# Attention layer with key and value products first and one query split; opening with zero matmuls, row-block products, half weights and stacked gate halves

## The chip, the cores and the metric

The kernel runs on one core of a Trainium2 chip. The metric is the device time of one execution in microseconds (us). TensorE is called PE below (PEld is its loading of weights), VectorE DVE, ScalarE ACT, GpSimd POOL and SyncE SP.

## The reference: a decoder trunk of two layers

x is 512 tokens of 1024 numbers, float32. Layer 1 is a gated linear attention (GLA, 4 heads of 128 keys and 256 values, in chunks of 64 tokens), layer 2 an attention with 16 heads of 64 in 4 groups. Each is followed by a feed-forward of 2 x 2816 with a short convolution. Cut to what the change touches:

```python
hn = rmsnorm(x, norm_mix[0])
q, k, v, r, a_low = split(hn @ gla_w_in)
log_a = log_sigmoid(a_low @ w_alpha_up + b_alpha) / 16   # a_low: 16 wide
b = cumsum(log_a)                                        # inside each chunk
state = state * exp(b_last) + (k * exp(b_last - b)).T @ v
o = (q * exp(b)) @ state + decayed causal attention inside the chunk
x = x + (rmsnorm(o) * silu(r)) @ w_o
x = x + conv_ffn(rmsnorm(x))

kv = (rmsnorm(x, kv_norm) @ w_kv)                 # 6 sets of 4 groups x 64
k_cmp = gelu(blocks(kv[0]) @ wk1) @ wk2           # 31 blocks of 32 tokens
v_cmp = gelu(blocks(kv[1]) @ wv1) @ wv2
k_sel, k_win = rope(kv[2]), rope(kv[4]);  v_sel, v_win = kv[3], kv[5]

hn = rmsnorm(x, norm_mix[1])
q = hn @ w_q;  gates = sigmoid(hn @ w_g)          # 3 gates per head
x = x + (gates[0] * o_cmp + gates[1] * o_sel + gates[2] * o_win) @ w_o
x = x + conv_ffn(rmsnorm(x));  return rmsnorm(x, norm_final)
```

The two norms ahead of the second attention are of the same x and differ only in their gain.

## The kernel before

**Numbers.** x stands transposed in `xall`, as eight tiles of 128 features x 512 tokens. To keep float32 precision, every operand of a product is split into two parts that PE takes in one pass each: a rounded one (`w_h`, `x_h`; made by ACT) and the rest (`w_l`, `x_l`; by DVE). A product of a 128-column weight with x is then 24 matmuls of 128x512: high by high, low by high, high by low, for each of eight tiles (`mm3`, L222; `proj`, L228; `proj_tok`, L236, has tokens on the partitions). `load_w` (L143) fetches and splits a weight. The gain of a norm is put into x when it is split (`split_x`, L161). The factor 1/rms is applied to the product's result (`rb`, a row spread over all partitions), so products start before the norm is known: `squares` (L188) makes and adds the squares, `rms_cols` sums them over partitions with PE (into `pc`), and `rms_behind` (L211) lets one product run while that is under way.

**Opening and GLA** (`gla`, L354). SP issues all loads: first columns of gains, x tile 0, the decay weight `gla_a` (16 columns), x tiles 1 to 4, the key weight of head 0, x tiles 5 to 7, its query weight, constants `kc`. The decay product `pa` (16 columns, 24 matmuls) and the key product `pk` of head 0 run tile by tile as x comes. ACT and POOL share the squares of this first norm (POOL multiplies those of odd tiles); in the later norms POOL makes the adds of the first tiles. `alow` (16 x 512) times `wup` (16 x 512, one 128-column piece per head) gives `pz`, the log of the decay before the sigmoid, as a plain float32 product, which PE takes in two passes (L383). `head_in` (L381) makes the decay `g`, its running sums `cum`, `k` and `q` of a head; `head_att` (L406) the attention in a chunk; `v_head` (L515) the values with `v_h` and `v_l`. L564 to L592 order the heads.

**Second attention** (`nsa_att`, L612). Its schedule is written out by hand (L901 to L945). x is split by the gain of the query norm (`mix1`), two query products run, x is split again by `kv`; then come rope of query pair 0 (`queries`, L659: SP copies halves over, the copies `q_s` are made by four DMAs), the gates, the rotated keys (`keys_in`, L678), the raw keys and values (`raw_in`, L754, which makes the blocks `kb`), the compression of both (`compress`, L704), scores of head 0, and the values by token (`values_in`, L692; `pvt`, `V`). Then x is split by `mix1` a second time for the later queries. `compressed` (L769) is the compressed branch of a group (`pC`, `pcm`, `smc`), `compressed_t` (L791) transposes its weights, `scores` (L799) has maxima `nm` and exponentials `p_t`, `values` (L854) transposes `p_t` and multiplies by V. In the loop over 16 heads, the scores of head h+1 are interleaved with the values of head h.

**Order.** The code is traced in this order; each engine takes its instructions in order, apart from `tc.high_priority` (moves a piece ahead by an offset) and `tc.issue_after` (not before a given instruction of the same engine). Tiles of one tag share a small ring of buffers (`TAGS`, L51), so that a write waits for the readers of the tile before. The core of the hand-written schedule:

```python
query()
xk = [split_x("kv")]
queries(0)
gates()
keys_in(0)
query()
raw_in(0)
keys_in(1)
raw_in(1)
raw_in(2)
raw_in(3)
compress("k")
compress("v")
run(scores(0))
```

## Time and profile before

| | |
|---|---|
| median of 3 runs | 1347.9 us (1347.73 to 1348.26) |
| profiled execution, its own time | 1346.67 us |
| its span | 1344.9 us |
| PE busy | 98%, 6592 instructions |
| DVE, ACT, POOL busy | 68%, 46%, 13% |
| DMA | 119.79 MB, mean 89 GB/s |

The span runs from the first to the last instruction that the profiler saw; the execution's own time is 1.8 us longer. A matmul's recorded duration covers its way through a pipeline, so two in a row overlap: the time that one costs on a full PE is the distance between two starts. A share of busy time is an average over the whole span; which wait ends last in a stage is read from that stage's rows in order of time.

### The profile page before, as it was taken

What the parts mean: (1) busy time and instruction counts of PE and PEld (TensorE: products, weight loads), DVE (VectorE), ACT (ScalarE), POOL (GpSimd) and SP (SyncE); (2) the same over time, 40 slices, a digit from 0 to 9 for tenths busy, and PEclk for the clock granted to TensorE, in tenths of its full rate; (3) what the DMA queues carried; (4) which work ended last, traced back from release to release, by engine and by line L of the source; (5) the groups of instructions that cost most, each with busy time, mean ns of one, the idle gap of its engine ahead of it and who ended that gap; (6) DMA issues with size and microseconds to landing.
All of it is one profiled execution on the core that took longest, in us unless ns stands there. A gap on an engine that the chain in (4) does not pass through costs nothing. (4 is left out here: it accounts for less than half of the span.)

```text
span 1344.9 us, 17502 instructions
## 1 busy us (share of the span) xinstructions
PE 1316.5 (98%) x6592; PEld 1079.7 (80%) x6592; DVE 911.4 (68%) x1414; ACT 620.4 (46%) x1036; POOL 168.6 (13%) x236
## 2 busy tenths in 40 slices
PE   8999999999999999999989999999999999999997
PEld 4988988888888888887779777777788888888886
DVE  6877765477636763765875898998767735773672
ACT  5444543344314431444446687776644413441342
POOL 3000001100000000002413444442200000000000
PEclk9999999999999999999999999999999999999999
DMA  5222213333333333334452211111333333332331
GB/s 185 73 63 64 63 48 94 95 94 94 94 94 94 98 102 95 94 83 150 121 174 72 65 39 36 48 52 32 112 94 100 103 94 94 94 94 95 94 110 63
DMA packets 40261, 119.79 MB, mean 89 GB/s; under 512 B 5344, under 2 KB 6240, under 8 KB 40176
## 3 DMA queue, kind: packets, MB, share of 16 engines
q1 hardware_dynamic: 39600, 117.62, 29.0%
q8 instruction: 52, 0.85, 0.3%
q10 hardware_dynamic: 576, 1.05, 0.2%
q14 instruction: 33, 0.27, 0.1%
HBM read 109.21 MB, written 2.10 MB: 83 GB/s over the span
## 5 line engine op out<-in xcount | busy, mean ns | idle before, releaser
L149 ACT ACTIVATE w_h<-w_raw 128x1024 fp32r<-128x1024 f32 (+3 forms) x198 | 200.1, 1011 | 307.1 <-PE pd L226 129.9
L224 PE MATMUL pu<-x_h,w_h 128*128 128x512 f32 x704 | 274.1, 389 | 0.0
L225 PE MATMUL pu<-x_h,w_l 128*128 128x512 f32 x704 | 274.1, 389 | 0.0
L226 PE MATMUL pu<-x_l,w_h 128*128 128x512 f32 x704 | 273.9, 389 | 0.0
L151 DVE TENSOR_TENSOR w_l<-w_raw,w_h 128x1024 fp32r<-128x1024 f32 (+3 forms) x184 | 220.0, 1196 | 49.9 <-ACT w_h L149 48.0
L224 PEld LDWEIGHTS pu<-x_h,w_h 128*128 128x128 f32 x704 | 132.1, 188 | 27.5
L226 PEld LDWEIGHTS pu<-x_l,w_h 128*128 128x128 f32 x704 | 132.1, 188 | 27.4
L225 PEld LDWEIGHTS pu<-x_h,w_l 128*128 128x128 f32 x704 | 132.1, 188 | 27.4
L224 PE MATMUL pd<-m_h,w_h 128*128 128x512 f32 x304 | 120.2, 395 | 0.0
L226 PE MATMUL pd<-m_l,w_h 128*128 128x512 f32 x304 | 120.1, 395 | 0.0
L225 PE MATMUL pd<-m_h,w_l 128*128 128x512 f32 x304 | 120.0, 395 | 0.0
L273 DVE TENSOR_TENSOR u<-pu,rb 128x512 f32<-128x512 f32 x88 | 60.6, 689 | 81.3 <-PE pu L226 77.4
L251 DVE TENSOR_TENSOR xall<-xall,pd 128x512 f32<-128x512 f32 x40 | 27.5, 688 | 100.8 <-PE pd L226 100.8
L272 POOL MEMSET u<- 128x2 f32 x88 | 8.4, 99 | 602.5 <-DVE cv L278 602.5
L156 ACT ACTIVATE m_h<-cv 128x512 fp32r<-128x512 f32 x44 | 27.8, 632 | 115.2 <-DVE cv L281 115.2
L275 ACT ACTIVATE cv<-u,cols 128x512 f32<-128x512 f32 x88 | 71.1, 808 | 2.7 <-DVE u L273 1.9
L826 ACT ACTIVATE p_t<-sc,nm 128x128 f32<-128x128 f32 (+3 forms) x128 | 66.8, 527 | 11.0 <-DVE nm L819 7.5
L224 PEld LDWEIGHTS pd<-m_h,w_h 128*128 128x128 f32 x304 | 57.1, 188 | 14.0 <-ACT m_h L156 0.4
L226 PEld LDWEIGHTS pd<-m_l,w_h 128*128 128x128 f32 x304 | 57.1, 188 | 13.9 <-DVE m_l L158 0.2
L278 DVE SCALAR_TENSOR_TENSOR cv<-u,cols,cv 128x512 f32<-128x512 f32 x88 | 66.2, 752 | 3.0
L225 PEld LDWEIGHTS pd<-m_h,w_l 128*128 128x128 f32 x304 | 57.1, 188 | 13.7
L277 DVE SCALAR_TENSOR_TENSOR cv<-u,cols,cv 128x512 f32<-128x512 f32 x88 | 65.7, 746 | 3.6 <-ACT cv L275 3.4
(284 smaller groups left out, 2661.5 us busy)
## 6 DMA issues: line engine op xcount, KB each, us to landing
w_raw<-in_ffn_up_dram SPq DMA_DIRECT2D x88, 512.0 KB, 3.6
w_raw<-in_ffn_down_dram SPq DMA_DIRECT2D x32, 512.0 KB, 3.5
w_raw<-in_gla_v_dram SPq DMA_DIRECT2D x8, 512.0 KB, 3.6
w_raw<-in_gla_r_dram SPq DMA_DIRECT2D x8, 512.0 KB, 3.5
w_raw<-in_gla_o_dram SPq DMA_DIRECT2D x8, 512.0 KB, 3.6
w_raw<-in_nsa_q_dram SPq DMA_DIRECT2D x8, 512.0 KB, 3.6
w_raw<-in_kv_f_dram SPq DMA_DIRECT2D x8, 512.0 KB, 3.8
q_s<-q_s SPq DMA_DIRECT2D x32, 128.0 KB, 2.2
```

What stands on the lines that cost most here:

```text
L149: ACT.activation(h, raw, AF.Copy)
L151: (POOL if pool else DVE).tensor_tensor(l, raw, h, OP.subtract)
L156: ACT.activation(h, src, AF.Copy)
L224: MM.append(PE.matmul(ps, wh, xh, start=first, stop=False).ins)
L225: PE.matmul(ps, wl, xh, start=False, stop=False)
L226: PE.matmul(ps, wh, xl, start=False, stop=last)
L251: DVE.tensor_tensor(xT[d], xT[d], ps, OP.add)
L273: DVE.tensor_tensor(u[:, 2:], ps, rb[0], OP.mult)
L275: ACT.activation(c, u[:, 2:2 + S], AF.Identity, scale=col(w, 3 * jj + 2), bias=col(f"conv_b{layer}", jj))
L277: DVE.scalar_tensor_tensor(c, u[:, 1:1 + S], col(w, 3 * jj + 1), c, OP.mult, OP.add)
L278: DVE.scalar_tensor_tensor(c, u[:, 0:S], col(w, 3 * jj), c, OP.mult, OP.add)
L826: ACT.activation(pr[i, b], scv[:, bi], AF.Exp, bias=nm[:, i, b:b + 1], accum_out=su[:, i, b:b + 1])
```

## The change

**Opening.** Three loads go to ACT's own queue ahead of its table load: the gains and the first halves (four row blocks) of the key and query weights of head 0. The rest stays on SP, with the second halves ahead of x tile 4 and the constants last, and four copies of the decay weight `w_alpha` at partitions 0, 32, 64, 96. Fourteen bf16 matmuls of zeros, 128x512, into the tile `pc` come first on PE. The products go by row block: for each x tile, those of the decay, of the key of head 0 and of its query. The decay weight is stacked to 112 columns (three copies of its high part and, at 96, its low part), so that `pa` takes two matmuls for each tile in place of three; `alow` and `wup` are stacked to match, and `pz` is one matmul of one pass over 112 rows. The key product of head 1 follows, and `rb` is spread behind its second block. All squares are made by ACT and all their adds by DVE, in every norm.

On PE, in the opening before the change (`pa` the decay product, `pk` that of the keys of head 0):

```order
L225 MATMUL pa<-x_h,w_l 16x512
L226 MATMUL pa<-x_l,w_h 16x512
L224 MATMUL pk<-x_h,w_h 128x512
L224 MATMUL pa<-x_h,w_h 16x512
L225 MATMUL pa<-x_h,w_l 16x512
L225 MATMUL pk<-x_h,w_l 128x512
L226 MATMUL pk<-x_l,w_h 128x512
```

And now, behind the zero matmuls (`pk_137` and `pq_138` are keys and queries of head 0):

```order
L393 MATMUL pa<-x_h,wa 112x512
L393 MATMUL pa<-x_l,wa 112x512
L230 MATMUL pk_137<-x_l,wk_h 128x512
L228 MATMUL pq_138<-x_h,w_h 128x512
L229 MATMUL pq_138<-x_h,w_l 128x512
L230 MATMUL pq_138<-x_l,w_h 128x512
L393 MATMUL pa<-x_h,wa 112x512
```

The decay product has one matmul fewer per tile, and the query product, which stood behind the norm, is now part of the same sweep over x.

On DVE, where the inputs of heads 0 and 1 are made, before (`alow` the decay's low-rank part, `g` the decay, `cum` its sums; the second `g` is that of head 1):

```order
L375 TENSOR_TENSOR alow<-pa,rb 16x512
L400 TENSOR_TENSOR k<-pk,rb 128x512
L390 TENSOR_SCALAR g<-pz,cols 128x512
L403 SCALAR_TENSOR_TENSOR q<-pq,rb 128x512
L151 TENSOR_TENSOR w_l<-w_raw,w_h 128x1024
L391 TENSOR_TENSOR g<-g,e 128x512
L395 SCALAR_TENSOR_TENSOR cum<-scan_174,g 128x512
L395 SCALAR_TENSOR_TENSOR cum<-scan_177,g 128x512
L395 SCALAR_TENSOR_TENSOR cum<-scan_180,g 128x512
L390 TENSOR_SCALAR g<-pz,cols 128x512
```

And now:

```order
L413 TENSOR_TENSOR alow_f<-pa,rb 112x512
L445 TENSOR_TENSOR k<-pk_137,rb 128x512
L448 SCALAR_TENSOR_TENSOR q<-pq_138,rb 128x512
L420 TENSOR_TENSOR alow<-alow_f,alow 16x512
L445 TENSOR_TENSOR k<-pk,rb 128x512
L155 TENSOR_TENSOR w_l<-w_raw,w_h 128x1024
L435 TENSOR_SCALAR g<-pz,cols 128x512
L436 TENSOR_TENSOR g<-g,e 128x512
L440 SCALAR_TENSOR_TENSOR cum<-scan_319,g 128x512
L440 SCALAR_TENSOR_TENSOR cum<-scan_322,g 128x512
L440 SCALAR_TENSOR_TENSOR cum<-scan_325,g 128x512
```

`q` of head 0, `k` of head 1 and a low part of a weight now stand ahead of the first `g`.

**Second attention.** x is split by the `kv` gain first. All products of keys and values are made from it (raw, compressed keys, rotated keys, values by token), and then x is split once by `mix1`, for gates and queries. The compression of the values, the gates and the second query product stand behind that. `compressed_t(0)` is moved into the first head.

On DVE, around the last split of x, before (`V_5060` one of the two value tiles, `pcm` and `smc` the softmax of the compressed branch, `nm`, `su` and `p_t` that of head 0):

```order
L697 SCALAR_TENSOR_TENSOR V_5061<-pvt,rc,V_5061 128x4x64
L778 TENSOR_TENSOR pcm<-pC,kc 128x512
L781 TENSOR_REDUCE mx<-pcm 128x16
L819 TENSOR_REDUCE nm<-sc 128x2 x2
L168 SCALAR_TENSOR_TENSOR x_l<-xall,cols,x_h 128x512
L819 TENSOR_REDUCE nm<-sc 128x1
L785 TENSOR_REDUCE smc<-pcm 128x16
L168 SCALAR_TENSOR_TENSOR x_l<-xall,cols,x_h 128x512
L786 RECIPROCAL smc<-smc 128x16
```

And now:

```order
L742 SCALAR_TENSOR_TENSOR V_5090<-pvt,rc,V_5090 128x4x64 x3
L172 SCALAR_TENSOR_TENSOR x_l<-xall,cols,x_h 128x512 x3
L155 TENSOR_TENSOR w_l<-w_raw,w_h 128x1024
L172 SCALAR_TENSOR_TENSOR x_l<-xall,cols,x_h 128x512 x4
L742 SCALAR_TENSOR_TENSOR V_5089<-pvt,rc,V_5089 128x4x64
L155 TENSOR_TENSOR w_l<-w_raw,w_h 128x384
L742 SCALAR_TENSOR_TENSOR V_5089<-pvt,rc,V_5089 128x4x64 x2
L172 SCALAR_TENSOR_TENSOR x_l<-xall,cols,x_h 128x512
L699 SCALAR_TENSOR_TENSOR qn<-sc,rb 128x512
```

The parts of x stand between copies of values and parts of weights, and no softmax work is among them.

The diff, cut:

```diff
+WARM = 14
...
     xall = const.tile([128, KT, S], F32, name="xall")
     xT = [xall[:, k] for k in range(KT)]
-    ACT.preload_act_table_set("natural_log_exp_and_others")
     pre = [T([128, 8, n], F32, "w_raw") for n in (16, 128, 128)]
     kc = const.tile([128, 128 + 128 + 128 + 1], F32, name="kc")
+    for dst, src in ((cols[:, 0:NGAIN], a["cols"][:, 0:NGAIN]), (pre[1][:, 0:4], a["gla_k"][0][:, 0:4]),
+                     (pre[2][:, 0:4], a["gla_q"][0][:, 0:4])):
+        nc.scalar.dma_start(dst, src)
+    ACT.preload_act_table_set("natural_log_exp_and_others")
     for dst, src in ((xT[0], a["xT"][0]), (pre[0], a["gla_a"]), (xT[1], a["xT"][1]), (xT[2], a["xT"][2]),
-                     (xT[3], a["xT"][3]), (xT[4], a["xT"][4]), (pre[1], a["gla_k"][0]), (xT[5], a["xT"][5]),
-                     (xT[6], a["xT"][6]), (xT[7], a["xT"][7]), (pre[2], a["gla_q"][0]), (kc, a["kc"]),
+                     (xT[3], a["xT"][3]), (pre[1][:, 4:8], a["gla_k"][0][:, 4:8]),
+                     (pre[2][:, 4:8], a["gla_q"][0][:, 4:8]), (xT[4], a["xT"][4]), (xT[5], a["xT"][5]),
+                     (xT[6], a["xT"][6]), (xT[7], a["xT"][7]), (kc, a["kc"]),
                      (cols[:, NGAIN:], a["cols"][:, NGAIN:])):
         nc.sync.dma_start(dst, src)
...
-    def load_w(src, shape, raw=None, pool=False):
+    def load_w(src, shape, raw=None, pool=False, prio=300):
         if raw is None:
             raw = T(shape, F32, "w_raw")
             nc.sync.dma_start(raw, src)
-        with tc.high_priority(offset=300):
+        with tc.high_priority(offset=prio):
...
-    def squares(first=False):
+    SQ = []
+
+    def squares():
         acc = None
         for k in range(KT):
-            sq = T([128, S], F32, "sq0" if first else "sq")
-            if first and k % 2:
-                POOL.tensor_tensor(sq, xT[k], xT[k], OP.mult)
-            else:
-                ACT.activation(sq, xT[k], AF.Square)
+            sq = T([128, S], F32, "sq")
+            last = [ACT.activation(sq, xT[k], AF.Square).ins]
             if acc is not None:
-                (POOL if k < 6 and not first else DVE).tensor_tensor(sq, sq, acc, OP.add)
+                last.append(DVE.tensor_tensor(sq, sq, acc, OP.add).ins)
             acc = sq
+        SQ[:] = last
         return acc
...
-        wa, wk, wq = (load_w(None, [128, 8, 128 if i else 16], t) for i, t in enumerate(pre))
-        xs = split_x("mix0")
-        acc = squares(first=True)
...
+        with tc.high_priority(offset=300):
+            zero = T([128, S], BF, "zero")
+            DVE.memset(zero, 0.0)
+            idle = P("pc")
+            for _ in range(WARM):
+                PE.matmul(idle, zero[:, 0:128], zero, start=True, stop=True)
+
+        was = [T([128, 4, 112], F32R, "wa") for _ in range(2)]
+        for wa in was:
+            POOL.memset(wa.bitcast(F32), 0.0)
+        wup_f = T([112, S], F32, "wup_f")
+        POOL.memset(wup_f, 0.0)
+        for o in range(0, 112, 32):
+            nc.sync.dma_start(wup_f[o:o + 16], a["w_alpha"])
+        wk, wq = ([T([128, 8, 128], F32R, n + x) for x in "hl"] for n in ("wk_", "w_"))
+        pa, pk0, pq0 = (P(n) for n in ("pa", "pk0", "pq0"))
+        xs = []
+        for k in range(KT):
+            xs += split_x("mix0", (k,))
+            if k % 4 == 0:
+                for raw, (h, l) in zip(pre[1:], (wk, wq)):
+                    ACT.activation(h[:, k:k + 4], raw[:, k:k + 4], AF.Copy)
+                    DVE.tensor_tensor(l[:, k:k + 4], raw[:, k:k + 4], h[:, k:k + 4], OP.subtract)
+                    if k == 0 and raw is pre[1]:
+                        for i, wa in enumerate(was):
+                            w3 = bass.AP(tensor=wa.tensor, offset=wa.offset,
+                                         ap=[list(wa.ap[0]), list(wa.ap[1]), [32, 3], [1, 16]])
+                            half = pre[0][:, 4 * i:4 * i + 4]
+                            ACT.activation(w3, half[:, :, None, :].to_broadcast([128, 4, 3, 16]), AF.Copy)
+                            DVE.tensor_tensor(wa[:, :, 96:112], half, wa[:, :, 0:16], OP.subtract)
+        acc = squares()
+        r4 = rms_cols(acc)
+        for k in range(KT):
+            for x in xs[k]:
+                PE.matmul(pa[0:112], was[k // 4][:, k % 4], x, start=k == 0 and x is xs[0][0], stop=k == KT - 1 and x is xs[k][1])
+            for ps, (wh, wl) in ((pk0, wk), (pq0, wq)):
+                mm3(ps, (wh[:, k], wl[:, k]), xs[k], k == 0, k == KT - 1)
+        first = len(MM)
+        pk1 = proj(None, xs, "pk", w=load_w(a["gla_k"][1], [128, 8, 128], prio=0))
+        with tc.high_priority(offset=100), tc.issue_after(MM[first + 1]):
+            rb = spread(r4, "rb")
...
-        wup = T([16, S], F32, "wup")
-        nc.sync.dma_start(wup, a["w_alpha"])
...
-        pa = proj(None, xs, "pa", w=wa, m=16)
-        rb, r4 = rms(acc)
-        al = T([16, S], F32, "alow")
-        DVE.tensor_tensor(al, pa[0:16], rb[0:16], OP.mult)
+        al_f = T([112, S], F32, "alow_f")
+        DVE.tensor_tensor(al_f, pa[0:112], rb[0:112], OP.mult)
+        wup = T([112, S], F32R, "wup")
+        with tc.issue_after(SQ[0]), tc.issue_after(SQ[1]):
+            ACT.activation(wup, wup_f, AF.Copy)
+            DVE.tensor_tensor(wup[32:48], wup_f[32:48], wup[32:48], OP.subtract)
+        al = T([112, S], F32R, "alow")
+        ACT.activation(al, al_f, AF.Copy)
+        DVE.tensor_tensor(al[64:80], al_f[64:80], al[64:80], OP.subtract)
...
-            pk = proj(a["gla_k"][h], xs, "pk", w=wk if h == 0 else None)
+            pk = proj(a["gla_k"][h], xs, "pk") if h > 1 else (pk0, pk1)[h]
             k = T([128, S], F32, "k")
             DVE.tensor_tensor(k, pk, rb, OP.mult)
-            pq = proj(a["gla_q"][h], xs, "pq", w=wq if h == 0 else None)
+            pq = proj(a["gla_q"][h], xs, "pq") if h else pq0
             q = T([128, S], F32, "q")
             DVE.scalar_tensor_tensor(q, pq, 128 ** -0.5, rb, OP.mult, OP.mult)
...
-        xq = [split_x("mix1")]
+        xk = split_x("kv")
         acc = squares()
-        early = [proj(a["nsa_q"][0], xq[0], "tp")]
-        rb, r4, ps = rms_behind(acc, lambda: proj(a["nsa_q"][1], xq[0], "tp"))
-        early.append(ps)
+        first = [proj(a["kv_f"][0], xk, "sc")]
+        rb, r4, ps = rms_behind(acc, lambda: proj(a["kv_f"][1], xk, "sc"))
+        first.append(ps)
...
-            ps = early[len(Q)] if len(Q) < 2 else proj(a["nsa_q"][len(Q)], xq[0], "pl", pool=True)
+            ps = proj(a["nsa_q"][len(Q)], xq, "pl" if len(Q) > 1 else "sc", pool=len(Q) > 1)
...
-            ps = proj(a["kv_f"][f], xk[0], "sc")
+            ps = proj(a["kv_f"][f], xk, "sc") if f > 1 else first[f]
...
+        for f in range(4):
+            raw_in(f)
+        keys_in(0)
+        compress("k")
+        keys_in(1)
+        values_in(1)
+        values_in(0)
+        xq = split_x("mix1")
         query()
-        xk = [split_x("kv")]
+        compress("v")
+        gates()
+        query()
         queries(0)
-        gates()
-        keys_in(0)
-        query()
-        raw_in(0)
-        keys_in(1)
-        raw_in(1)
-        raw_in(2)
-        raw_in(3)
-        compress("k")
-        compress("v")
         run(scores(0))
         queries(1)
-        values_in(1)
-        values_in(0)
-        xq[0] = split_x("mix1")
         compressed(0)
         query()
-        compressed_t(0)
         for h in range(16):
             gs = scores(h + 1) if h + 1 < 16 else None
             if h % 4 == 2 and h < 14:
                 compressed(h // 4 + 1)
             gv = values(h)
-            for c in INTERLEAVE:
+            for n, c in enumerate(INTERLEAVE):
+                if h == 0 and n == 6:
+                    compressed_t(0)
                 if c == "v":
...
```

## Rows read from the trace of the kernel before

**Rows 1.** The page's first part: busy time, share of the span, instructions.

```profile
PE 1316.5 (98%) x6592; PEld 1079.7 (80%) x6592; DVE 911.4 (68%) x1414; ACT 620.4 (46%) x1036; POOL 168.6 (13%) x236
```

**Rows 2.** Order of time, PE, opening: start, duration (us), line, operation.

```profile
5.08 0.61 PE L224 MATMUL pa<-x_h,w_h 128*16 128x512 f32 x1 [5.08 <-ACT w_h L149]
...
8.49 0.63 PE L225 MATMUL pa<-x_h,w_l 128*16 128x512 f32 x1
8.92 0.63 PE L226 MATMUL pa<-x_l,w_h 128*16 128x512 f32 x1
...
22.16 1.04 PE L204 MATMUL pc<-mean_d,sq 128*128 128x1 f32 x8
...
26.75 1.12 PE L383 MATMUL pz<-alow,wup 16*128 16x512 f32 x2
27.80 0.50 PE L225 MATMUL pq<-x_h,w_l 128*128 128x512 f32 x1
...
40.99 0.39 PE L226 MATMUL pq<-x_l,w_h 128*128 128x512 f32 x1
41.21 0.28 PE L224 MATMUL pv<-w_h,x_h 128*128 128x256 f32 x1
...
53.54 0.61 PE L438 MATMUL plv<-ev 128*128 128x128 f32 x4
...
56.53 0.39 PE L224 MATMUL pv<-w_h,x_h 128*128 128x256 f32 x1
```

**Rows 3.** PE's waits, 600 to 770 us: total, times, longest (us).

```profile
PE sc L815 <- DVE kb L759: 4.2, 1, 4.2
PE pl L224 <- ACT x_h L166: 1.6, 1, 1.6
PE sc L225 <- DVE w_l L151: 0.9, 1, 0.9
...
PE sc L226 <- DVE x_l L168: 0.5, 1, 0.5
```

**Rows 4.** Order of time, PE, attention stage; in brackets the idle time before it.

```profile
694.61 0.47 PE L815 MATMUL sc<-K,q_s 128*128 128x512 f32 x1 [4.23 <-DVE kb L759]
```

**Rows 5.** Windows: PE, PEld, DVE, ACT, POOL busy (instructions), PE clock, DMA share, GB/s.

```profile
28.63:56.44 27.81, 27.25 (x171) 23.93 (x169) 23.21 (x41) 13.60 (x24) 0.00 (x0) 1.00 0.25 76
695.00:700.00 5.00, 5.00 (x31) 4.85 (x30) 3.55 (x10) 1.74 (x3) 0.00 (x0) 0.66 0.77 266
746.70:960.00 213.30, 208.29 (x1195) 158.96 (x1194) 186.72 (x374) 156.33 (x391) 81.50 (x73) 1.00 0.17 44
```

**Rows 6.** SP's issue of the constants, its landing (page's DMA issues), x_l in the opening.

```profile
6.91 0.70 SPq L122 DMA_DIRECT2D kc<-in_kc_dram  x1
...
kc<-in_kc_dram SPq DMA_DIRECT2D x1, 192.5 KB, 7.0
...
L168 DVE SCALAR_TENSOR_TENSOR x_l<-xall,cols,x_h x8: 737/752/1523, 4.9 to 14.9; 128x512 fp32r<-128x512 f32 x8
```

**Rows 7.** Order of time, DVE, opening: the adds of squares and g of head 0.

```profile
19.09 3.01 DVE L197 TENSOR_TENSOR sq<-sq,sq 128x512 f32<-128x512 f32 x4
...
28.63 0.75 DVE L390 TENSOR_SCALAR g<-pz,cols 128x512 f32<-128x512 f32 x1 [1.48 <-ACT e L386]
```

**Rows 8.** The page's costliest groups: total busy, mean ns of one, idle before.

```profile
L151 DVE TENSOR_TENSOR w_l<-w_raw,w_h 128x1024 fp32r<-128x1024 f32 (+3 forms) x184 | 220.0, 1196 | 49.9 <-ACT w_h L149 48.0
```

**Rows 9.** Query 0: DVE's qn, SP's four issues of q_s, their landing (page).

```profile
630.90 0.69 DVE L654 SCALAR_TENSOR_TENSOR qn<-tp,rb 128x512 f32<-128x512 f32 x1 [2.86 <-ACT rb L178]
...
639.48 5.08 SPq L671 DMA_DIRECT2D q_s<-q_s  x4
...
q_s<-q_s SPq DMA_DIRECT2D x32, 128.0 KB, 2.2
```

**Rows 10.** The chain that ended last, 665 to 688 us: a slow rope's first and last piece.

```profile
667.59 0.70 DVE kx L682
...
683.41 0.61 DVE rot L632
```

More of the change, by code (lines that the diff above doesn't have):

```diff
@@ L48 @@
                ("conv_w0", 132), ("conv_w1", 132), ("conv_b0", 44), ("conv_b1", 44)])
-TAGS = {"sq0": "y1", "x_h": "xs", "x_l": "xs", "kx": "pt_h", "gz": "pt_h", "lo": "sq", "o_t": "sq", "w2": "sq", "qn": "qo", "o_h": "qo", "o_l": "qo", "kb": "qo",
+TAGS = {"sq0": "y1", "x_h": "xs", "x_l": "xs", "zero": "rv", "wa": "ev", "wk_h": "ah", "wk_l": "al", "wup_f": "sqo", "alow_f": "sqo", "pk0": "po", "pq0": "po", "kx": "pt_h", "gz": "pt_h", "lo": "sq", "o_t": "sq", "w2": "sq", "qn": "qo", "o_h": "qo", "o_l": "qo", "kb": "qo",
         "pz": "ps", "pvt": "tp", "pqk": "ps", "plv": "ps", "pc": "pn", "pb": "pn", "pgt": "pn", "pC": "pn", "pT": "pn",
@@ L111, in tile_kernel @@
     cols = const.tile([128, NCOLS], F32, name="cols")
-    nc.sync.dma_start(cols[:, 0:NGAIN], a["cols"][:, 0:NGAIN])
     xall = const.tile([128, KT, S], F32, name="xall")
     xT = [xall[:, k] for k in range(KT)]
-    ACT.preload_act_table_set("natural_log_exp_and_others")
     pre = [T([128, 8, n], F32, "w_raw") for n in (16, 128, 128)]
     kc = const.tile([128, 128 + 128 + 128 + 1], F32, name="kc")
+    for dst, src in ((cols[:, 0:NGAIN], a["cols"][:, 0:NGAIN]), (pre[1][:, 0:4], a["gla_k"][0][:, 0:4]),
+                     (pre[2][:, 0:4], a["gla_q"][0][:, 0:4])):
+        nc.scalar.dma_start(dst, src)
+    ACT.preload_act_table_set("natural_log_exp_and_others")
     for dst, src in ((xT[0], a["xT"][0]), (pre[0], a["gla_a"]), (xT[1], a["xT"][1]), (xT[2], a["xT"][2]),
-                     (xT[3], a["xT"][3]), (xT[4], a["xT"][4]), (pre[1], a["gla_k"][0]), (xT[5], a["xT"][5]),
-                     (xT[6], a["xT"][6]), (xT[7], a["xT"][7]), (pre[2], a["gla_q"][0]), (kc, a["kc"]),
+                     (xT[3], a["xT"][3]), (pre[1][:, 4:8], a["gla_k"][0][:, 4:8]),
+                     (pre[2][:, 4:8], a["gla_q"][0][:, 4:8]), (xT[4], a["xT"][4]), (xT[5], a["xT"][5]),
+                     (xT[6], a["xT"][6]), (xT[7], a["xT"][7]), (kc, a["kc"]),
                      (cols[:, NGAIN:], a["cols"][:, NGAIN:])):
@@ L159, in split, with split_x @@
         return h, l
-    def split_x(gain):
+    def split_x(gain, ks=range(KT)):
         xs = []
-        for k in range(KT):
+        for k in ks:
             g = col(gain, k)
@@ L637, in gates @@
         def gates():
-            pg = proj(a["nsa_g"], xq[0], "po", m=48)
+            pg = proj(a["nsa_g"], xq, "po", m=48)
             gz = T([48, S], F32, "gz")
@@ L679, in keys_in @@
             for ft in range(2):
-                ps = proj(a["kv_f"][4 + 2 * br + ft], xk[0], "sc")
+                ps = proj(a["kv_f"][4 + 2 * br + ft], xk, "sc")
                 k = T([128, S], F32, "kx")
@@ L692, in values_in @@
         def values_in(br):
-            pv = proj_tok(a["kv_v"][br], xk[0], "pvt")
+            pv = proj_tok(a["kv_v"][br], xk, "pvt")
             for i in range(4):
```

## The prediction

> **What bounds the kernel now.** I read the page's first part, then the view of waits, then TensorE's rows in order of time, then the windows. The page shows TensorE (PE) busy for 98% of the span [rows 1], so a gain needs PE work removed or a PE pause closed; what other engines do counts where PE waits for it. Three places matter to this change. In the **opening**, PE has its first product at 5.08 us, and products of 512 columns start 0.43 us apart there (8.49, 8.92), against 0.22 to 0.23 later (40.99, 41.21), which is the 2.4 GHz level; the slow step is the 1.2 GHz level, after 5 us with nothing to do [rows 2]. The value products of head 0 start at 41.21. In the **attention stage**, the view of waits names 4.2 us for kb, 1.6 us for x_h, 0.9 for w_l and 0.5 for x_l [rows 3]; the first is one hole of 4.23 us that ends at 694.61 [rows 4]. Behind that hole the granted clock averages 0.66 over 695 to 700 [rows 5]: a share s at half speed gives 1 - s/2 = 0.66, so s = 0.68, or 3.4 us at half speed, which costs 1.7 us more. The feed-forward stages show no PE wait that the change touches.
>
> **The change part by part.**
>
> *Opening, PE.* The fourteen zero products wait for one clear on VectorE alone; I let them start at 1.1 us, a guess that shifts the sum by its own error only. In the old kernel the slow stretch lasted from 5.08 to past 8.92, ten products [rows 2]; ten zeros at 0.43 and four at 0.23 end near 6.3. From there the eight row blocks (two for the decay, three for k, three for q) are 64 products of 0.23, and the mean-square product has its slot after 61 of them: 6.3 + 14.0 = 20.3. Whether PE gets there without holes depends on x. More weights now stand ahead of the last x tile, but the constants behind them all landed by 13.9 in the old kernel (next paragraph but one), with the same bytes ahead, and PE wants the last tile only at 6.3 + 7 x 1.8 = 18.9. If zeros did nothing for the clock, ten real products would pay 0.2 us more each, 2.0 in all.
>
> The Trainium skill, "TensorE: Matmul & The Clock Gate", section "What's actually happening", says that the number of slow products at the start varies from run to run, with 6, 11 and 14 in one kernel. No run here shows such a spread; by that rule the zeros end between 5.5 and 7.1 instead of at 6.3, which would move the opening by under a microsecond either way.
>
> *Opening, VectorE.* This queue is the later one. All seven adds of squares are now on DVE, none of the squares is made on POOL, and the three casts of the constants stand in front of x_l of tile 5. Those constants landed 7.0 us after their issue at 6.91 [rows 6], at 13.9; the bytes ahead of them are the same now, so I keep 13.9 and let the casts end at 14.4. Behind them stand three x_l of 0.75 [rows 6], six adds of 0.75 (four took 3.01 [rows 7]) and one w_l of 1.2 [rows 8]: 14.4 + 2.3 + 4.5 + 1.2 = 22.4. The mean-square product starts there and not at 20.3; the hole is 2.1 us.
>
> From that product (22.16 in the old kernel) to the value products at 41.21 was 19.05 us. The new one has 14 full products fewer in it (51 for 65), 3.2 us, and two decay products in one pass: the old one takes 1.05 us, 26.75 to 27.80 [rows 2], the new one 0.23, so 0.8 less each. That is 19.05 - 3.2 - 1.6 = 14.2, and the values start at 36.6, 4.6 us earlier. k of head 1 now stands ahead of the scans, and with it goes the old pause inside the values: they took 12.33 us, 41.21 to 53.54, for 96 products of 256 columns, 11.5 at half a product each and a little. PE would be 4.6 + 0.8 = 5.4 us earlier at 53.54.
>
> It keeps less than that. At 56.53 PE takes a value product whose buffer comes free with the second v_l [rows 2]. Between g at 28.63 [rows 7] and that v_l's end at 56.44, DVE was busy 23.21 of 27.81 us [rows 5]. Two w_l (2.4) and one k and one q (1.4) are moved ahead of g, which leaves 19.4, with 0.9 of waits for ScalarE's exponentials 20.3. g itself comes 1.9 us behind the first decay product (at 26.75 before; now 24 products and two decay products ahead of the values, 36.6 - 5.5 - 0.5 = 30.6), at 32.5, so the second v_l ends at 52.8 and PE is 3.6 us ahead at that mark. **I take 3.6**; the bounds are 2 (constants or x land 2 us later) and 7 (the constants land early, and DVE is not late).
>
> *Decay products of heads 2 and 3.* 0.8 us each on a full PE: **1.6**. The copies for the stacked halves lie on ScalarE and DVE beside PE work and cost nothing while DVE keeps its slack: 23.21 of 27.81 us.
>
> *Adds of squares in the later norms* (POOL to DVE, five adds at 0.75 in each of three norms): hidden; PE is full of output products while each x tile waits for its sum. Without that cover it would be 3.8 us each.
>
> *Attention stage.* The raw key and value products come first, so each kb has a whole product of 5.5 us (24 x 0.23) before its buffer is wanted again, and the blocks are formed long before the compression reads them. That closes the 4.2 us hole and the 1.7 of slow clock behind it. One of three splits of x is gone, which removes the x_l wait of 0.5. The remaining split follows the last value product, with no softmax work queued between its parts; the query product takes 5.5 us to come to the tile that is split last. That closes the 1.6 for x_h. The 0.9 for w_l came from a DVE queue full of rope and kb work, which is now spread out. Sum 8.9.
>
> New waits: the value products of the second pair want both buffers, freed by four copies that ScalarE and DVE do beside 3 us of compression products: an estimated 0.5. The first scores lost their cover, the value products. Query 0 now ends about 17.5 us of PE work before the scores (gates 5.5, compression 4.4 and its second product 1.7, query 1 5.5, transpositions 0.4). The old chain from qn at 630.90 to the last copy of q_s, issued by 644.56 and landing 2.2 us later, was 15.9 us [rows 9]: it fits by 1.6, and the first head needs only half the copies. Between scores and first transposition stands the third query, 5.0 us, where DVE has maxima, sums and scalings; I put 1.5 on that start. With 0.5 and 1.5 the stage gives **6.9**; the bounds are 1 (the new waits cost 8) and 10.5 (none, and the small pauses of the old start go as well).
>
> **Sum.** 3.6 + 1.6 + 6.9 = 12.1. The profiled execution took 1346.67 (span 1344.9, 1.8 around it): 1334.6. The median of the runs, 1347.9, is 1.2 above that execution, so 1335.8.
>
> **Rivals.**
> - *The opening gives nothing but shorter products.* DVE stays late through all of head 0 (in its favour: it is in order, and I already find it 2 us behind PE twice; against: it has 4.6 us of slack in that window). Opening 0.5 for 3.6: 1338.9.
> - *The attention stage only moves its pauses.* Rope copies, softmax of the first head and the transposition of the compressed weights stop PE for 7 us in place of 2: 1335.8 + 5 = 1340.8. For it: a rope of the old stage took from 667.59 to 683.41 [rows 10], 15.8 us against 7.2 for the first one, when copies stood behind other transfers. Against: SP has fewer large transfers around query 0.
> - *Slower: the first head runs bare.* If query 0's rope is as slow as that one, PE stops 8.6 - 1.6 = 7 us ahead of the scores, pays 1.7 for the clock behind it, and then waits for a whole head of DVE work, 186.72 / 16 = 11.7 us [rows 5], with none of it covered: 20.4. The gains without any new wait are 3.6 + 1.6 + 8.9 = 14.1, so the kernel would be 6.3 slower, 1354.2. It decides from 14.1 us of pauses between the last value product and the first transposition.
> - *Both parts whole*, the upper bounds: 7 + 1.6 + 10.5 = 19.1, 1328.8.
> - *The zeros do not do what they are there for*: 2.0 more, 1337.8, inside the forecast's own range.
>
> **How the numbers follow.** The forecast gets 0.60 with the zeros' case in it (its own range 1331 to 1340), the opening's rival 0.14, the attention stage's 0.15, both whole 0.07, the bare head 0.04. A measurement of this kernel can tell 0.2%, 2.7 us, from no change. All but the last case are faster than 1345.2; the attention rival with the opening's on top, 1335.8 + 3.1 + 5 = 1343.9, is near it, so I give 0.93 to faster, 0.03 to the same and 0.04 to slower. The range runs from the case with both parts whole, 1328.8, to both rivals together, 1343.9.
>
> **What would show it.** Right: slow steps only among the zero products; the mean-square product near 22 with a hole of 1 to 2 us before it; value products of head 0 near 36.5; a wait on v_l soon after; no wait for kb and a granted clock of 1.0 through the attention stage; less than 3 us of PE waits around the first scores. Wrong: holes of PE between row blocks (x too late), waits for q_s or p_t of more than 5 us at the first head, or a new DVE wait in the norms.

## The result, and the profile after

The changed kernel takes 1338.59 us in the median of four runs (1336.01 to 1339.27), the kernel before 1348.03 (1347.73 to 1348.26): a ratio of 0.9929, 95% interval 0.9917 to 0.9941, so 9.4 us less. 1335.8 was predicted, with a range of 1328.8 to 1343.9. The profiled execution took 1339.27, 7.4 less than that of before (1346.67). The 2 us between these two differences come from which executions were profiled: that of before lies 1.4 us under its median, that of the changed kernel 0.7 above its own.

The page's first part, which answers to [rows 1]:

```profile
PE 1315.6 (98%) x6594; PEld 1084.1 (81%) x6594; DVE 910.2 (68%) x1427; ACT 610.8 (46%) x1030; POOL 138.2 (10%) x220
```

PE is as busy as before; as said ahead, its share tells nothing here. PE's rows in order of time in the opening answer to [rows 2]:

```profile
1.19 6.10 PE L364 MATMUL pc<-zero 128*128 128x512 bf16 x14 [1.19 <-DVE mhalf L141]
6.78 0.74 PE L228 MATMUL pk<-x_h,wk_h 128*128 128x512 f32 x1
7.35 0.39 PE L229 MATMUL pk<-x_h,wk_l 128*128 128x512 f32 x1
7.58 0.39 PE L393 MATMUL pa<-x_h,wa 128*112 128x512 f32 x1
...
21.19 0.94 PE L208 MATMUL pc<-mean_d,sq 128*128 128x1 f32 x8
...
34.67 0.28 PE L228 MATMUL pv<-w_h,x_h 128*128 128x256 f32 x1
...
46.18 0.61 PE L483 MATMUL plv<-ev 128*128 128x128 f32 x4
...
52.44 0.58 PE L228 MATMUL pv<-w_h,x_h 128*128 128x256 f32 x1 [3.11 <-DVE v_l L568]
```

The real products run at steps of 0.23 us from the second on, with no hole between row blocks. The values of head 0 start at 34.67 (before 41.21), `plv` follows at 46.18 (53.54): PE is 7.4 us ahead. Then it waits 3.1 us for the second `v_l` and goes on at 52.44 (56.53), 4.1 ahead. The windows show what comes behind that hole; the columns are those of [rows 5], the stretches 47 to 62 us and 737 to 742:

```profile
47.00:62.00 15.00, 11.89 (x78) 11.61 (x77) 10.69 (x24) 5.30 (x11) 0.00 (x0) 0.77 0.22 69
...
737.00:742.00 5.00, 4.25 (x19) 3.23 (x19) 3.23 (x8) 4.41 (x15) 4.20 (x4) 0.66 0.33 80
```

The granted clock, a mean over its two levels of 1.2 and 2.4 GHz, falls to 0.77, which by the prediction's reckoning, (1 - 0.77) x 15, costs up to 3.5 us. The lead shows 2.6 of it: by the value product that started at 59.62 in the old kernel and now at 58.15, PE is 1.5 us ahead. At head 2's decay product it still is (72.17 for 73.66), and behind it 2.3; behind head 3's it grows again, from 2.54 to 3.36. At the first product of the feed-forward stage it is 3.5 (253.30 for 256.81), behind the attention stage 7.5 (936.74 for 944.27, an output product at its end). PE's rows at these marks, before and then now:

```profile
73.66 1.12 PE L383 MATMUL pz<-alow,wup 16*128 16x512 f32 x2
...
256.81 0.39 PE L224 MATMUL pu<-x_h,w_h 128*128 128x512 f32 x1
...
944.27 0.48 PE L226 MATMUL pw<-o_l,w_h 128*128 128x512 f32 x1
```

```profile
72.17 0.40 PE L428 MATMUL pz<-alow,wup 112*128 112x512 f32 x1
...
253.30 0.39 PE L228 MATMUL pu<-x_h,w_h 128*128 128x512 f32 x1
...
936.74 0.48 PE L230 MATMUL pw<-o_l,w_h 128*128 128x512 f32 x1
```

PE's waits between 600 and 770 us, which answer to [rows 3]:

```profile
PE sc L860 <- ACT p_t L871: 2.7, 1, 2.7
PE ph L769 <- DMA w1b<-in_cmp_w1k_dram: 1.5, 1, 1.5
PE tp L917 <- DVE pt_l L921: 0.4, 1, 0.4
PE pk L793 <- DVE gr L789: 0.2, 1, 0.2
```

The hole for `kb` [rows 4] and the waits for x are gone. So are two that [rows 3] leaves out:

```profile
PE pgt L643 <- DVE gz L640: 0.6, 1, 0.6
PE pl L226 <- DVE x_l L168: 0.4, 1, 0.4
```

Two others stand in their place: 1.5 us for a weight of the compression, `w1b`, and 2.7 for the score buffer of head 1, which is freed by ACT's exponentials `p_t`; the second window above is what follows this one, 0.66 over 5 us, or 1.7 us.

### The profile page after: what moved, and what is told of

Same layout as the page of the kernel before. It is cut to its first block, busy times and chain, and to the rows that moved or that the text cites. A ratio compares the mean times of both kernels' runs of the same rounds, so it can differ in the third digit from the quotient of the medians.

```text
span 1337.5 us, 17491 instructions
## 1 busy us (share of the span) xinstructions
PE 1315.6 (98%) x6594; PEld 1084.1 (81%) x6594; DVE 910.2 (68%) x1427; ACT 610.8 (46%) x1030; POOL 138.2 (10%) x220
## 4 chain that ended last, share of the span: by engine, by line
PE 86%; DVE 9%; issue 2%; POOL 1%; ACT 1%; DMA 0%; SPq 0%; POOLq 0%; DVEq 0%; ACTq 0%
PE pu L228 12%; PE pu L229 12%; PE pu L230 12%; PE pd L228 6%; PE pd L230 6%; PE pd L229 6%; PE pw L230 2%; PE pw L228 2%; PE pw L229 2%; DVE p_t L891 2%; PE plv L541 2%; PE po L909 2%; PE tp L917 2%; DVE pt_l L921 1%; DVE nm L864 1%
## 5 line engine op out<-in xcount | busy, mean ns | idle before, releaser
L153 ACT ACTIVATE w_h<-w_raw 128x1024 fp32r<-128x1024 f32 (+2 forms) x195 | 197.8, 1014 | 328.8 <-PE pd L230 129.9
L155 DVE TENSOR_TENSOR w_l<-w_raw,w_h 128x1024 fp32r<-128x1024 f32 (+3 forms) x181 | 216.5, 1196 | 51.7 <-ACT w_h L153 49.6
```

The lines of the kernel that those rows point to most:

```text
L153: ACT.activation(h, raw, AF.Copy)
L155: (POOL if pool else DVE).tensor_tensor(l, raw, h, OP.subtract)
```

## Experiments

The kernels ran in three groups, each beside the kernel before (medians 1347.86, 1348.01 and 1348.04). The changed kernel itself ran in the first of them and, for the result, ahead of them; where a later run is set against it, both its medians, 1338.59 and 1339.48, are meant. The first four runs ask which part is worth what.

**The changed kernel again, without an edit.**

> The changed kernel as it is, to see how far its executions lie apart and whether the waits of its first trace come back. First theory (the waits are fixed by the order of the instructions): again a PE wait of about 3 us for v_l, 2.7 us for the buffer of the second head's scores and 1.5 us for w1b, and times within 1 us of 1338.6. Rival (one of the waits hangs on when transfers land, and comes and goes): times 2 to 3 us apart, as 1336.0 and 1339.3 were, and one of the three waits shorter by that much in this trace.

1339.48 us (1337.88 to 1340.34), ratio 0.9934 (0.9921 to 0.9948). The three waits came back with 3.1, 2.7 and 2.0 us, so the order makes them; the first theory holds for their places. The times lie 2.5 us apart, as the rival had it. The price of the waits differs: the clock over 47 to 62 us was 0.89 and not 0.77, and this time 0.93 over 640 to 665, behind `w1b`, where the first trace has 1.00. What comes and goes is mostly the slow clock behind a hole.

```profile
47.00:62.00 15.00, 11.87 (x86) 11.59 (x85) 11.50 (x27) 5.53 (x13) 0.00 (x0) 0.89 0.23 70
```

**The opening alone**, and **the attention stage alone**. The edits are the two halves of the diff shown ahead (up to `head_in`, and from `nsa_att` on); the first line of each:

```diff
-        wa, wk, wq = (load_w(None, [128, 8, 128 if i else 16], t) for i, t in enumerate(pre))
...
-        xq = [split_x("mix1")]
+        xk = split_x("kv")
```

> The kernel before with the change of the opening, the decay products and the squares alone; the attention stage is the old one. As predicted: 3.6 + 1.6 = 5.2 us less than before, about 1342.8. By the trace of the changed kernel (PE 7.3 us ahead at the values of head 0, of which the wait for v_l and the slow clock behind it leave 1.5, and 1.7 from the decay products of heads 2 and 3): about 3.5 less, 1344.5. Rival (the parts are not additive, and the opening gains only with the new attention stage): under 2 less.

> The kernel before with the new order of the attention stage alone. As predicted: 6.9 us less than before, about 1341.1. By the trace of the changed kernel (7.75 us ahead behind the stage, 3.5 of them from the opening): 4.2 less, about 1343.8, with the same 2.7 us wait for the buffer of the second head's scores and 1.5 us for w1b. Rival (the median of the changed kernel lies 9.4 under before, its profiled execution 7.4: the attention stage is worth more in other executions): 5.5 to 6 less.

1343.27 us (ratio 0.9965, 0.9952 to 0.9977) and 1343.41 (0.9966, 0.9954 to 0.9979): 4.6 and 4.4 us less than before, together 9.0, where the whole change gave 9.4 and 8.4. The parts add up, so the rivals of both fall. The opening lies near the predicted 5.2; the attention stage lies 2.5 short of its 6.9.

**Without the zero products.**

```diff
-            idle = P("pc")
-            for _ in range(WARM):
-                PE.matmul(idle, zero[:, 0:128], zero, start=True, stop=True)
```

> The changed kernel without the fourteen zero products. Theory (zeros bring PE to its fast clock ahead of the real products, and VectorE's queue starts from the first decay product, so all of it is passed on): ten to fourteen real products at the slow step of 0.43, the mean-square product about 2 us later than 21.2, and the kernel 2 us slower. Rival (VectorE's lateness hides it: PE waits for v_l anyway): the mean-square product 2 us later, but the wait for v_l shorter by as much, and the time the same within 0.5.

1340.41 us (1340.09 to 1343.08), ratio 0.995 (0.9938 to 0.9963), against 1339.48 for the changed kernel on the same chip: 0.9 more, within the spread of both. PE's rows in order of time show where it comes from (those at 9.95 and 10.24 are the ninth and the tenth product):

```profile
5.80 0.80 PE L228 MATMUL pk<-x_h,wk_h 128*128 128x512 f32 x1 [5.80 <-ACT wk_h L377]
...
9.95 0.46 PE L390 MATMUL pa<-x_h,wa 128*112 128x512 f32 x1
10.24 0.39 PE L390 MATMUL pa<-x_l,wa 128*112 128x512 f32 x1
...
21.32 0.95 PE L208 MATMUL pc<-mean_d,sq 128*128 128x1 f32 x8
...
35.66 0.28 PE L228 MATMUL pv<-w_h,x_h 128*128 128x256 f32 x1
...
53.42 0.39 PE L228 MATMUL pv<-w_h,x_h 128*128 128x256 f32 x1 [3.11 <-DVE v_l L565]
```

Eight products run slowly, but they start at 5.80 and not behind the zeros at 6.78. The mean-square product is only 0.1 us later, since it has come four places forward in PE's order (57 products ahead of it for 61). The values show the loss: they start at 35.66, for 34.67 in the first trace of the changed kernel and 34.00 to 35.22 in all seven traces with its opening. The 3.1 us wait for `v_l` is unchanged and ends as much later (53.42 for 52.44). So the loss is passed on, as the theory had it, and no shorter wait hides it; but it is about 1 us and not 2. What neither theory had: in the first trace PE is busy with zeros until 6.78, although the first weights are there by 6.10, where DVE goes on with them (in two of the eleven traces with zeros PE waits for them all the same, 0.35 and 0.45 us).

The Trainium skill, "TensorE: Matmul & The Clock Gate", section "What's actually happening", has the number of slow products at the start vary from run to run. The traces agree: the opening of the old kernel has nine full slow steps in the trace of before (5.08 to 8.92; the prediction's tenth is slow in part) and sixteen, up to the row shown here, in that of the attention stage alone, which has the same opening. The fourteen zeros were reckoned at 5.2 us; to the first real product it is 4.7 to 5.6 in the eleven traces.

```profile
13.32 0.63 PE L224 MATMUL pk<-x_h,w_h 128*128 128x512 f32 x1
```

The next runs ask what the three waits come from.

**Low parts of five weights on POOL.**

```diff
-        pv = proj_tok(a["gla_v"][hd], xs, "pv")
+        pv = proj_tok(a["gla_v"][hd], xs, "pv", pool=hd < 2)
...
+            pq = proj(a["gla_q"][h], xs, "pq", pool=h == 1) if h else pq0
```

> The changed kernel with five low parts of weights in the opening (query weight of head 1, both halves of the value weights of heads 0 and 1) made by POOL, which has nothing to do there, in place of VectorE. Theory (the wait for v_l comes from VectorE's queue alone, which stands full from g to v_l): three of these parts, 1.2 us each, stand between g and the second v_l and one ahead of g, so the 3.1 us wait goes, and with it the slow clock behind it (0.50 and 0.72 over 52 to 58 us in two traces, 1.7 to 3 us at half speed); 3 to 4.5 us less than the changed kernel. Rival (the low parts come too late from POOL, at about 2.4 us each, and PE waits for w_l in place of v_l): under 1 us less, or slower.

1340.92 us (ratio 0.9948, 0.9936 to 0.9961): no gain, and the wait for `v_l` grew to 4.3 us. DVE has five instructions of 1.2 us fewer and is later. POOL's rows of that kernel, 36 to 48 us, and behind them DVE's in the same stretch:

```profile
37.60 2.40 POOL L155 TENSOR_TENSOR w_l<-w_raw,w_h 128x1024 fp32r<-128x1024 f32 x1 [4.99 <-ACT w_h L153]
43.42 3.20 POOL L155 TENSOR_TENSOR w_l<-w_raw,w_h 128x1024 fp32r<-128x1024 f32 x1 [3.42 <-ACT w_h L153]
```

```profile
37.87 2.67 DVE L436 TENSOR_TENSOR g<-g,e 128x512 f32<-128x512 f32 x1
...
41.77 0.41 DVE L480 TENSOR_TENSOR ev<-ev,q 128x256 f32<-128x256 f32 x1
...
44.35 2.55 DVE L479 TENSOR_TENSOR ev<-ev,k 128x256 f32<-128x256 f32 x1
```

The same `g` took 0.68 and the same `ev` 0.40 in the changed kernel. Both start while POOL is in one of its parts and end 0.5 and 0.3 us behind it. Instructions that read one of their tensors from PSUM kept their time beside a POOL part (`alow_f`, `k` and `q` with 0.68 to 0.69 beside one of 24.27 to 26.68). Moving work off a full DVE in this way gave it back with interest: 2.0 and 2.1 us lost for two parts of 1.2 saved.

The Trainium skill, "SBUF — State Buffer", section "Who interferes with whom", has a DVE instruction with two SBUF inputs contend with a POOL instruction that reads SBUF; it calls the ports that the two share an exclusive lock and lets the order of issue decide who is held up. The trace agrees (2.67 for 0.68, begun 0.27 us behind POOL's part).

**The parts of the first values earlier in the queue.** Nothing is taken away; `v_h` and `v_l` of head 0 get a higher priority, and the factors of the chunk levels from m = 2 on stand behind the second `v_l`.

```diff
+                    with tc.high_priority(offset=1000 if hd == 0 else 0):
                         ACT.activation(h[:, cs], pv[b][:, cs], AF.Copy, scale=r4[:, i:i + 1])
...
+                    if h == 0 and li > FREE:
+                        after_v = tc.issue_after(VL[0, 1])
+                        after_v.__enter__()
```

> The changed kernel with the low and high parts of the first values (v_h, v_l of head 0) put ahead of the chunk products' factors (levels from m = 2 on) in the queues of VectorE and ACT, no work taken away or moved to POOL. Theory (the 3.1 us wait is a place in a queue: the second v_l stands behind some dozen short instructions and a low part of a weight): v_l lands 2 to 4 us earlier, the wait is under 1 us, the slow clock behind it goes, 2.5 to 4.5 us less than the changed kernel (about 1334 to 1336.5). Rival (the factors that now come later are waited for as much): waits for ev, qf or kf at the first chunk products take its place, under 1 us less.

1334.27 us (1333.44 to 1335.5), ratio 0.9901 (0.9888 to 0.9913): 4.3 to 5.2 us less than the changed kernel. DVE's rows of the changed kernel show what had stood ahead of the second `v_l` (the values are done on PE at 46.2):

```profile
46.99 0.43 DVE L533 TENSOR_TENSOR kf<-k,ev 128x256 f32<-128x256 f32 x1 [0.51 <-ACT ev L529]
47.33 0.42 DVE L538 TENSOR_TENSOR qf<-ev,q 128x256 f32<-128x256 f32 x1
...
49.37 0.42 DVE L533 TENSOR_TENSOR kf<-k,ev 128x256 f32<-128x256 f32 x1 [0.83 <-ACT ev L529]
49.71 0.48 DVE L568 SCALAR_TENSOR_TENSOR v_l<-pv,rc,v_h 128x256 fp32r<-128x256 f32 x1
...
50.77 1.22 DVE L155 TENSOR_TENSOR w_l<-w_raw,w_h 128x1024 fp32r<-128x1024 f32 x1
51.91 0.87 DVE L568 SCALAR_TENSOR_TENSOR v_l<-pv,rc,v_h 128x256 fp32r<-128x256 f32 x2
```

None of the factors is wanted by PE before the pair of `v_l` is. With the new order PE has no wait there, and the window of that kernel shows PE full and the clock whole:

```profile
47.00:62.00 15.00, 15.00 (x128) 14.85 (x126) 13.68 (x32) 6.92 (x14) 0.00 (x0) 1.00 0.31 102
```

PE reaches the feed-forward stage at 247.71, 9.1 us ahead of the old kernel in place of 3.5. The wait was a place in a queue; no wait for a factor took its place.

**Rotated keys earlier.**

```diff
-        for f in range(4):
-            raw_in(f)
-        keys_in(0)
+        raw_in(0)
+        raw_in(1)
+        keys_in(0)
+        raw_in(2)
+        raw_in(3)
```

> The changed kernel with the first rotated keys made behind the second raw product and no longer behind the fourth, ahead of the compression. Theory (the load of w1b shares buffers with the tile kx of the rotated keys and stands behind its copies in SP's queue, so it is issued at 652.3 and lands too late): the load is issued some 10 us earlier, the 1.5 to 2.0 us wait and any slow clock behind it go, 1.5 to 3 us less, and times that lie closer together. Rival (with fewer products ahead of the compression PE waits for the blocks or for kb): the wait turns into one for kb or blk of 1 us or more, and the time is the same.

1336.44 us (1334.89 to 1337.49), ratio 0.9915 (0.9901 to 0.9929): 2 to 3 us less than the two medians of the changed kernel. SP's rows, first of the changed kernel, then of this one:

```profile
649.11 2.52 SPq L673 DMA_DIRECT2D sw<-kx  x4
651.74 0.52 SPq L150 DMA_DIRECT2D w_raw<-in_kv_v_dram  x1
652.29 1.23 SPq L766 DMA_DIRECT2D w1b<-in_cmp_w1k_dram  x2
```

```profile
636.21 2.73 SPq L673 DMA_DIRECT2D sw<-kx  x4
639.04 0.53 SPq L150 DMA_DIRECT2D w_raw<-in_kv_f_dram  x1
639.61 1.19 SPq L766 DMA_DIRECT2D w1b<-in_cmp_w1k_dram  x2
```

The load of `w1b` goes out behind the copies of `kx`, wherever these are; 12.7 us earlier, it is on time. The wait is gone, and no wait for a block came. The times, 2.6 us apart, lie no closer together than before, so that part of the theory failed. (Whether it is the queue's order or the shared buffers that hold the load was not told apart.)

**Softmax of the compressed branch later.**

```diff
         queries(1)
-        compressed(0)
         query()
...
-                if h == 0 and n == 6:
-                    compressed_t(0)
+                if h == 0 and n == 3:
+                    compressed(0)
...
+            if h == 0:
+                compressed_t(0)
             run(gv)
```

> The changed kernel with the compressed branch of group 0 and its softmax put into the first head's loop and no longer ahead of it. Theory (PE waits 2.7 us for the score buffer of head 1 since VectorE has that softmax, 3.7 us, in its queue ahead of the maxima): the wait shrinks to under 1 us and the slow clock behind it (0.66 over 737 to 742) goes, 2 to 4 us less. Rival (VectorE is simply too full in the first head, whatever the order): the wait moves to the transposition of the compressed weights or to p_t, and the time is the same within 1 us.

1337.1 us (1335.73 to 1337.72), ratio 0.992 (0.9907 to 0.9934): 1.5 to 2.4 less. DVE's rows of the changed kernel have pieces of that softmax (`smc`) ahead of the maxima (`nm`) that ACT's exponentials wait for; PE went on at 737.75:

```profile
733.52 0.67 DVE L830 TENSOR_REDUCE smc<-pcm 128x16 f32<-128x512 f32 x1
...
735.73 0.81 DVE L833 TENSOR_SCALAR smc<-smc,kc 128x4 f32<-128x4 f32 x1
736.45 1.61 DVE L864 TENSOR_REDUCE nm<-sc 128x2 f32<-128x256 f32 x3
```

PE's longest waits of the kernel of this run, 700 to 770 us:

```profile
PE tp L917 <- DVE pt_l L921: 2.0, 2, 1.1
PE pT L839 <- POOL pcm L834: 0.6, 1, 0.6
```

The 2.7 us hole is gone; smaller ones have come, and the waits of the whole view add up to 3.2 us, where the changed kernel has 3.3. Both theories have a part of it: the hole hung on the order, and DVE is full in the first head. What was saved is the slow clock, 1.00 over 735 to 750 where the changed kernel has 0.89: holes of 1.1 us did not bring the clock down here.

**Together.** First the low parts on POOL, the earlier keys and the later softmax; then keys and softmax alone; then these two with the parts of the first values ahead in the queue. The edits are those above.

> The changed kernel with the three edits together. Theory (three separate pauses): the gains add up, 6 to 10 us less than the changed kernel, so about 1329 to 1333. Rival (what one closes opens another): less than the largest of the three alone.

> The changed kernel with the earlier rotated keys and the later softmax of the compressed branch, without the parts on POOL. Theory (two separate pauses, worth 2 to 3 and 1.5 to 2.4 us alone): both gains, 1334 to 1335. Rival (they share something, as the queue of VectorE in the first head): no more than the better of the two, 1336.4.

> The changed kernel with all three edits that add no work to POOL: parts of the first values first, rotated keys earlier, softmax later. Theory (three separate pauses): 1330 to 1332. Rival (a pause closed early in the program only leads to the next one): 1334 or more.

1338.26 us (ratio 0.993, 0.9918 to 0.9943): POOL's parts take back what the others give. 1335.61 (0.9922, 0.9909 to 0.9935; 1334.27 to 1340.62 in six runs): one gain and little of the second by the median, with two runs 4 to 6 us above the others (mean clock 0.994 and 0.993, the others 0.997 and 0.998), so that it shows no addition. 1331.83 (0.9883, 0.987 to 0.9896; 1330.89 to 1333.54): the version without a long hole beats both kernels, by 16.2 and by 6.8 to 7.7 us. Of its waits on PE up to 770 us none is longer than 1.0 us, but for the start.

The trace of the second of them holds a point on the clock. It has the same 3.1 us wait for `v_l`, and its window reads

```profile
47.00:62.00 15.00, 11.89 (x100) 11.58 (x99) 12.63 (x31) 6.92 (x14) 0.00 (x0) 1.00 0.24 70
```

**The adds of squares back on POOL** in the three later norms.

```diff
-                last.append(DVE.tensor_tensor(sq, sq, acc, OP.add).ins)
+                last.append((POOL if 0 < k < 6 and SQ else DVE).tensor_tensor(sq, sq, acc, OP.add).ins)
```

> The changed kernel with the first five adds of squares in the three later norms back on POOL, as in the old kernel. As predicted (hidden on either engine: PE has output products to do while each tile of x waits for its sum): the same within 0.5 us. Rival (a POOL instruction with two tensor inputs stops VectorE while it runs, as the low parts on POOL did in the opening, or VectorE is late there): 1 to 4 us more, or as much less.

1338.36 us (ratio 0.9929, 0.9917 to 0.9941), the ratio of the changed kernel to the last digit shown: no difference that the runs can tell. In the first of the three norms POOL's adds take 1.8 us each and begin behind DVE's parts of x, which keep their 0.74 us; PE has no wait there in either kernel.

## Why the prediction was right, and where it was off

**Opening, 3.6 predicted.** PE came further ahead (7.4 us at `plv` for 5.4). The constants landed 5.3 us after their issue and not 7.0, and DVE's parts of x and adds start 0.66 and 0.60 us apart where the sum took 0.75 for each; DVE was done with the adds at 20.4, so the mean-square product had no 2.1 us hole before it (21.19 for 22.4). From there to the values it was 13.5 us for 14.2. What holds PE afterwards was placed rightly, the time with some luck: the second `v_l` was reckoned to end at 52.8, and PE went on at 52.44, but `g` came at 31.20 and not at 32.5, and DVE took 21.2 us from there and not 20.3 (19.6 of them busy, for 19.4 reckoned). The step that failed is the one behind it. The prediction priced slow clock behind the old `kb` hole and none behind its own `v_l` hole. In seven traces with this opening (the kernels that move the parts of weights or values, and the one without zeros, are left out) that wait ends 3.5 to 4.8 us ahead of the old kernel, and at head 2's decay product 1.5, 2.5, 2.5, 3.0, 3.2, 3.3 and 3.6 of it are left. On the way from one to the other the trace whose clock stayed whole loses nothing, five lose 1.4 to 1.5 us, and the first 2.6. So 3.6 was near the price without slow clock, and about 3.0 the usual one. All this is set against one trace of the old kernel (see the last section); the run of the opening alone, 4.6 with the 1.6 of the decay products in it, gives 3.0 as well.

**Zeros.** 2.0 us was put on their failing. Taking them away costs about 1: 0.9 in the medians, which is within their spread, and 0.4 to 1.7 at the start of the values.

**Decay products of heads 2 and 3, 1.6 predicted.** 0.8 and 0.8 in the leads at the two products, 1.6.

**Squares' adds, nothing predicted.** The run with the adds on POOL shows no difference.

**Attention stage, 6.9 predicted; 4.4 by the run of it alone, 4.0 in the trace.** The closed pauses were right and a little low: the view of before has 8.4 us of waits between 600 and 770, which with 1.7 of slow clock is 10.1 for the 8.9 summed up. The step that failed is the new waits, put at 0.5 and 1.5: they came to 1.5 + 2.7 + 0.4, and 1.7 of slow clock with them, 6.3 for 2.0. The wait of the first head was 2.7 and not 1.5, and the 1.7 behind it was not in the sum. A full DVE between scores and scalings had been named as its cause; that the softmax of the compressed branch stands in that queue had not. The wait for `w1b` was not foreseen at all: the step that moved `keys_in` was followed on PE and DVE, not on SP's queue, where its copies stand ahead of the compression's weights. The value products' buffers, on which 0.5 was put, made no wait. The two errors of this part, closed pauses too low and new ones far too low, cancel only in part.

**The rivals.** "The attention stage only moves its pauses" asked for 7 us in place of 2; 6.3 with the slow clock counted, so by its size the truth lies nearer to it than to the forecast, with larger pauses closed. "The opening gives nothing but shorter products" put 0.5 on the opening; 3.0 were measured. "Slower" did not come: the first head's rope was in time, and no wait for `q_s` stands in the trace. Of the prediction's own signs of being right, three did not come: the hole before the mean-square product, a clock of 1.0 through the attention stage, and less than 3 us of waits around the first scores (2.7 + 0.4).

## What to carry to other kernels

Where PE is full, price a hole with the slow clock that may follow it, for the new holes of a change as for the old ones. A wait for an engine that is nearly full can be a matter of order, as it was here for `v_l`: look at what stands ahead of the awaited instruction and whether PE wants that sooner, before work is moved to another engine; POOL in particular can stop DVE for as long as its own instruction runs. When a step is moved, follow its transfers through the issuing queue as well, to the load that now stands behind them.

## What was not expected of the hardware

The same hole of 3.1 us, at the same place behind the same instructions, was followed by a granted clock of 0.77, 0.89 or 1.00 over 47 to 62 us (first trace; six others; the run with keys and softmax moved). The instructions up to there are the same in all eight, but for the zeros that one of them lacks, and what the clock took of the lead by head 2 is nothing, 1.4 to 1.5 us or 2.6. The runs of the changed kernel lie 3.3 and 2.5 us apart in its two groups, those of the kernel before 0.5 and 1.0. The slow clock is the likely reason, which was not tried by itself: of the first four runs the fastest, 1336.01 us, has a mean clock of 0.999 and the two slowest 0.995. The wait for `w1b`, 1.4 to 2.0 us where it stands, is not enough for it, since the times without it (rotated keys earlier) lie 2.6 us apart. The profiled execution of the changed kernel was the slowest of its four, with the lowest of the clocks over 47 to 62 us.

The old opening has this too. In the trace of the attention stage alone it runs with a clock of 0.66 over 31 to 36 us, with PE busy throughout and its last wait ended at 10.35, and reaches head 2's decay product 1.5 us later than in the trace of before (73.66); 0.7 of that stood already at the mean-square product (22.89 for 22.16). The leads told above are against the earlier of the two. Windows and PE rows of that trace:

```profile
31.00:36.00 5.00, 5.00 (x16) 3.98 (x16) 4.86 (x5) 2.79 (x7) 0.00 (x0) 0.66 0.32 105
```

```profile
75.19 1.12 PE L383 MATMUL pz<-alow,wup 16*128 16x512 f32 x2
```

The Trainium skill, "TensorE: Matmul & The Clock Gate", section "What's actually happening", tells of such a spread at a kernel's start; that it comes behind a hole as well, and once without one, is what the rows here add.

And a DVE instruction with two tensors in SBUF stood still while POOL worked on two: 0.40 us became 2.55. The kernel before had shown it: the slowest `x_l` of [rows 6], 1523 ns where the median is 752, starts at 12.78 us, inside a square of POOL that runs from 12.08 to 13.76.
